# Row maxima, GLA scores and SSD scores and state products as pairs of 64-row products on the two halves of TensorE's contraction rows

## The chip, the core and the metric

One core of one Trainium2 chip runs the whole program in one launch. The metric is the device time of one execution in microseconds (us). The time before is 1848.38 us, the median of 3 runs (1847.5 to 1854.49).

The core has a matrix engine (TensorE: PE for its products, PEld for the loads of its stationary operand), a vector engine (DVE), an activation engine (ACT), GpSimd (POOL), and a queue that issues most of the DMAs (SP). TensorE contracts over up to 128 partitions ("rows") and writes into PSUM, which has eight banks of 512 fp32 columns per partition.

## The reference

Two layers of a hybrid trunk are computed for 128 context tokens and 1024 latent tokens, nine tiles of 128 tokens in all. Each layer makes one wide input projection, feeds four head groups with it, concatenates their outputs and makes one output projection. Three of the groups matter here:

```python
# A: grouped-query attention, 4 query heads on 2 key heads, head dim 64
s = jnp.einsum('bqhgd,bkhd->bhgqk', qblk, k) * scale
p = jax.nn.softmax(s, axis=-1)
# B: gated linear attention (GLA), 4 heads, dk 32, chunked, one scan per direction
att = jnp.where(mask, jnp.einsum('bnihd,bnjhd->bnhij', q_dec, k_in), 0.0)
# D: Mamba-2 SSD, 4 heads in 2 groups, state 64, chunked, one scan per direction
scores = jnp.einsum('bnigs,bnjgs->bnijg', cc, bc)
y_intra = jnp.einsum('bnijg,bnijgr,bnjgrp->bnigrp', scores, decay_ij, xc)
y = jnp.einsum('bigs,bgrps->bigrp', c_n, h) * jnp.exp(cum_n)[..., None]   # state product
```

Group C is a latent attention (MLA) with four heads of width 96. A softmax does not change when the same number is taken from all scores of a row, so the number that stands in for the row's maximum need not be exact.

## The kernel before, in words

Per layer the program projects (the helpers `proj_tok` and `proj_T`, whose products all stand on L245), then runs an attention stage, then the output projection (also L245, tile `op`). In the projections each operand is split into a high and a low part in the type fp32r, three products for one.

The attention stage runs eight heads in turn, four GQA and four MLA. While head n goes through `attend` (score products `st` on L1057, exponentials on ACT, value products `po` on L1067 to L1073), the preparation of head n+1 is advanced in small steps. `STEPS` says how many steps belong to a head, and `paced` hangs each step behind the last instruction issued by `attend`. Part of the preparation is `maxima`. For every query tile of 128 tokens it multiplies the query tile with all 1280 keys in three products (512, 512 and 256 columns, L710, tile `mx`), and DVE reduces each product to a maximum (L711). Nine tiles make 25 products for one head, 200 for the GQA heads of both layers and 200 for the MLA heads. The GQA products contract over 128 rows: the high part of the query on 64 rows and its low part on the other 64, against the high part of the key, which stands twice in `KA`. Head 0 is prepared earlier, between the tiles of the last projection (`cons_qk`, tiles `psP`).

Beside the heads run four more streams, whose instructions are written before the heads: two GLA scans (`gla`), the SSD state scans (`ssd_states`) and the SSD outputs (`ssd_out`). For the four GLA heads of 32 rows each, POOL spreads the query into four masked copies (L853, `g_Qb`), and one 128-row product of 512 columns in plain fp32 makes the scores (L865, `att`); DVE copies them under the causal mask (L867). For the two SSD groups POOL masks `C` in two copies (L962, `d_cb`); one product of 256 columns makes the scores (L987, `dsc`), and two of 256 columns multiply `C` with the carried states of both directions (L996, `dyi`), which DVE scales (L1001) and POOL adds.

The order on each engine comes from a scheduler of the programming layer. It lays the instructions of all streams out before the run, by its own estimate of when each could start; on the chip every engine takes its own in that order. PSUM is given out by tags: `psA`, `psB` two banks each, `psC` one, `psD` three. The maxima of head 0 and all GLA and SSD products use `psD`, the other maxima `psA`.

Of the kernel before, what the change touches and what calls it, by code (L numbers as in the profile page):

```python
# [8 lines left out]
F32 = mybir.dt.float32  # L9
# [15 lines left out]
WO_AT, WO_N = 5, 5  # L25
STEPS = (13, 19, 13, 25, 22, 20, 19, 0)
EPS = 1e-6
# [7 lines left out]
def hybrid_trunk_kernel(ctx: ExitStack, tc: tile.TileContext, a):  # L35
# [53 lines left out]
    bm = const.tile([128, 256], F32, name="bm")  # L89
    hm = const.tile([128, 4], F32, name="hm")  # L90

# [242 lines left out]
    for l in range(L):  # L334
# [83 lines left out]
        with st1:  # L418
# [281 lines left out]
            def maxima(sets, mpass, mr, psX=psA):  # L700

                qb = sets[3]
                mx = mxp.tile([128, T, 3], F32, name="mx", tag="mx", bufs=2)
                lt_m, rh_m = mpass
                for t in range(T):
                    s = slice(t * 128, (t + 1) * 128)
                    cks = ((0, 128),) if t == 0 else ((128, 512), (640, 512), (1152, 256))
                    for i, (o, n) in enumerate(cks):
                        p = psX("mx")
                        pe.matmul(p[:, 0:n], lhsT=lt_m[:, s], rhs=rh_m[:, o:o + n], start=True, stop=True)  # L710
                        dve.tensor_reduce(out=mx[:, t, i:i + 1], in_=p[:, 0:n], axis=AX.X, op=ALU.max)  # L711
                    if t not in (0, 4, 8):
                        yield
                        continue
# [20 lines left out]
            def both(xs, ys):  # L735

                for _ in zip_longest(xs, ys):
                    yield

            def prep_gqa(h):  # L740
# [5 lines left out]
                rq = slice((h % 2) * 64, (h % 2) * 64 + 64)  # L746
                rq2 = slice(64 - (h % 2) * 64, 128 - (h % 2) * 64)
                q = qT[:, h // 2, :]
                eng = pool if h else dve

                def rest():
                    for x in QC:
                        act.copy(qb[0:64, x], q[rq, x])
                        yield
# [46 lines left out]
        with ExitStack() as sta:  # L801
# [25 lines left out]
            def gla(d):  # L827
# [3 lines left out]
                for n, t in enumerate([*(range(T - 1, 0, -1) if d else range(1, T)), 0]):  # L831
                    last = n == T - 2
                    if t == 0:
# [17 lines left out]
                                             op0=ALU.mult, op1=ALU.mult)  # L851
                    qb = W([128, 4, 128], f"g_Qb{d}")
                    pool.tensor_tensor(out=qb, in0=kq[:, 128:256].unsqueeze(1).to_broadcast([128, 4, 128]),  # L853
                                       in1=hm.unsqueeze(2).to_broadcast([128, 4, 128]), op=ALU.mult)
                    if not last:
# [11 lines left out]
                    dve.copy_predicated(A, mask[:, d, :].unsqueeze(1).to_broadcast([128, 4, 128]),  # L867
                                        p.rearrange("p (h i) -> p h i", i=128))
                    o = psD("go")
# [40 lines left out]

            gm = W([128, 2], "gm")
            sp.dma_start(out=gm, in_=a["gm"])

            def h_rows(t, d):
# [3 lines left out]
            def ssd_states(d):  # L918
# [5 lines left out]
                for t in [*(range(T - 1, 1, -1) if d else range(1, T - 1)), 0]:  # L924
# [7 lines left out]
                    if t == 0:  # L932
                        hs = W([128, 128], "d_hs", 1, tag="d_yi")
# [14 lines left out]
            def ssd_out():  # L948

                for t in (0, 4, 5, 3, 6, 2, 7, 1, 8):  # L950
# [5 lines left out]
                    sp.dma_start(out=sz, in_=d_sz[t])  # L956
                    Hs = []
                    for d in range(2 if t else 0):
                        Hs.append(W([128, 256], "d_Hb", 2))
                        sp.dma_start(out=Hs[d], in_=h_rows(t, d))  # L960
                    cb = W([128, 2, 128], "d_cb")
                    pool.tensor_tensor(out=cb, in0=bc[:, 1, :].unsqueeze(1).to_broadcast([128, 2, 128]),  # L962
                                       in1=gm.unsqueeze(2).to_broadcast([128, 2, 128]), op=ALU.mult)
                    for d, tr in enumerate((TRI_F, TRI_B)):
# [12 lines left out]
                    for h in range(4):  # L977
# [11 lines left out]
                    dve.tensor_tensor(out=Dm.rearrange("p (g r) i -> p g r i", r=2),  # L989
                                      in0=scp[:, 0:256].rearrange("p (g i) -> p g i", i=128).unsqueeze(2).to_broadcast([128, 2, 2, 128]),  # L990
                                      in1=Dm.rearrange("p (g r) i -> p g r i", r=2), op=ALU.mult)
                    yield
                    if t:
                        ip = psD("dyi")
                        for d in range(2):
                            pe.matmul(ip[:, d * 256:(d + 1) * 256], lhsT=bc[:, 1, :], rhs=Hs[d], start=(d == 0), stop=(d == 1),  # L996
                                      skip_group_check=True)
                        for d in range(2):
                            yi = W([128, 256], "d_yi")
                            e = d * 36 + t * 4  # L1000
                            dve.tensor_tensor(out=heads(yi), in0=heads(ip[:, d * 256:(d + 1) * 256]),  # L1001
                                              in1=ec[:, e:e + 4].unsqueeze(2).to_broadcast([128, 4, 64]), op=ALU.mult)
                            pool.tensor_tensor(out=y, in0=y, in1=yi, op=ALU.add)
                    yp = psD("dy")
# [108 lines left out]
            def prep_mla(h):  # L1113
# [65 lines left out]

                yield from both(maxima((ka, kb, qa, qb), (qb[0:96], ka[0:96]), 96), rest())  # L1180

# [125 lines left out]
def _constants(np):  # L1307
# [12 lines left out]
    hd = i // 32  # L1320
# [3 lines left out]
    def rope(rot):  # L1324
# [18 lines left out]
        "sel": np.tile(np.eye(2, dtype=np.float32), (2, 1)),  # L1343
        "hm": (hd[:, None] == np.arange(4)[None, :]).astype(np.float32),
        "gm": ((i // 64)[:, None] == np.arange(2)[None, :]).astype(np.float32),
        "rope": np.concatenate([c64, s64, c32, s32], axis=1),
# [89 lines left out]
```

## Time and profile before

| | us |
|---|---|
| median of 3 runs | 1848.38 (1847.5 to 1854.49) |
| profiled execution, its own time | 1848.65 |
| its span, first to last instruction | 1846.8 |
| PE busy | 1720.3 (93%) |
| DVE busy | 1191.8 (65%) |
| ACT busy | 867.2 (47%) |
| POOL busy | 740.6 (40%) |

Matmuls are pipelined: a product's row in the trace lasts from its start to the modelled end of its result, longer than it keeps the engine from the next one. What it costs the engine is the distance from its start to the start of the next. A plain fp32 product shows as two rows, an fp32r product as one.

### The profile page before, as it was taken

What the parts mean: (1) busy time and instruction counts of PE and PEld (TensorE: products, weight loads), DVE (VectorE), ACT (ScalarE), POOL (GpSimd) and SP (SyncE); (2) the same over time, 40 slices, a digit from 0 to 9 for tenths busy, and PEclk for the clock granted to TensorE, in tenths of its full rate; (3) what the DMA queues carried; (4) which work ended last, traced back from release to release, by engine and by line L of the source; (5) the groups of instructions that cost most, each with busy time, mean ns of one, the idle gap of its engine ahead of it and who ended that gap; (6) DMA issues with size and microseconds to landing.
All of it is one profiled execution on the core that took longest, in us unless ns stands there. A gap on an engine that the chain in (4) does not pass through costs nothing.

```text
span 1846.8 us, 25193 instructions
## 1 busy us (share of the span) xinstructions
PE 1720.3 (93%) x8200; PEld 1321.0 (72%) x8200; DVE 1191.8 (65%) x2302; ACT 867.2 (47%) x1914; POOL 740.6 (40%) x911
## 2 busy tenths in 40 slices
PE   6999989999999998999999999999999999999998
PEld 2787977887665666656777999889666666665676
DVE  7627888566877887782455357543686878677233
ACT  5634422433654665583443152232465477557322
POOL 4633238852444444330334323771344454333011
PEclk9999998999999999999999999999998999899999
DMA  8434453333332331142434332131332232114243
GB/s 290 134 97 139 140 158 90 106 111 99 109 99 73 87 97 49 38 149 60 143 118 129 99 101 86 56 101 43 111 117 84 68 98 86 46 38 149 80 143 114
DMA packets 179684, 190.99 MB, mean 103 GB/s; under 512 B 29406, under 2 KB 140720, under 8 KB 179552
## 3 DMA queue, kind: packets, MB, share of 16 engines
q1 hardware_dynamic: 174208, 179.11, 31.9%
q10 hardware_dynamic: 5344, 10.26, 1.8%
q8 instruction: 65, 1.06, 0.2%
q14 instruction: 67, 0.55, 0.1%
HBM read 141.00 MB, written 48.30 MB: 103 GB/s over the span
## 4 chain that ended last, share of the span: by engine, by line
PE 36%; DVE 11%; DMA 7%; POOL 4%; ACT 3%; issue 3%; SPq 0%; POOLq 0%; DVEq 0%; ACTq 0%
PE psP L245 11%; PE op L245 8%; PE st L1057 3%; PE po L1073 3%; DVE mx L711 2%; DMA R<-d_rec 2%; PE mx L710 1%; DVE Pl L1065 1%; DMA d_rec<-rc 1%; PE po L1069 1%; DMA wst<-in_w_in_dram 1%; PE po L1067 1%; PE po L1068 1%; POOL ss L107 1%; POOL sq L577 1%
## 5 line engine op out<-in xcount | busy, mean ns | idle before, releaser
L711 DVE TENSOR_REDUCE mx<-mx 128x1 f32<-128x512 f32 (+2 forms) x400 | 224.5, 582 | 93.6 <-PE mx L710 92.0
L245 PE MATMUL psP<-whi,hh 128*128 128x512 f32 (+2 forms) x576 | 204.9, 366 | 5.6 <-DVE whi L235 4.3
L245 PE MATMUL psP<-wlo,hh 128*128 128x512 f32 (+2 forms) x576 | 204.8, 363 | 3.4 <-POOL wlo L239 2.8
L245 PE MATMUL psP<-whi,hl 128*128 128x512 f32 (+2 forms) x576 | 188.4, 360 | 0.0
L239 POOL TENSOR_TENSOR wlo<-wst,whi 128x512 fp32r<-128x512 f32 (+3 forms) x106 | 128.9, 1224 | 141.5 <-DVE whi L235 82.4
L245 PE MATMUL psP<-hh,whi 128*128 128x384 f32 x480 | 163.0, 339 | 4.7 <-DVE whi L235 3.7
L1057 PE MATMUL st<-QA,KA 128*128 128x512 f32 (+1 forms) x336 | 165.2, 492 | 0.6 <-DVE Pl L1065 0.4
L245 PE MATMUL psP<-hl,whi 128*128 128x384 f32 x480 | 160.2, 335 | 0.0
L245 PE MATMUL psP<-hh,wlo 128*128 128x384 f32 x480 | 155.0, 337 | 0.1
L1065 DVE TENSOR_TENSOR Pl<-st,Ph 128x512 fp32r<-128x512 f32 x160 | 109.7, 686 | 67.2 <-ACT st L1063 66.0
L1062 ACT ACTIVATE Ph<-st 128x512 fp32r<-128x512 f32 x160 | 95.5, 597 | 111.2 <-PE st L1057 104.4
L1072 ACT ACTIVATE P<-st 128x512 f32<-128x512 f32 (+1 forms) x176 | 99.7, 567 | 74.4 <-PE st L1057 65.3
L1057 PE MATMUL st<-QB,KB 66*128 66x512 f32 (+3 forms) x336 | 133.2, 401 | 0.0
L245 PEld LDWEIGHTS psP<-wlo,hh 128*128 128x128 f32 x576 | 111.5, 195 | 21.3 <-POOL wlo L239 6.8
L245 PEld LDWEIGHTS psP<-whi,hh 128*128 128x128 f32 x576 | 111.6, 195 | 20.0 <-DVE whi L235 6.1
L245 PEld LDWEIGHTS psP<-whi,hl 128*128 128x128 f32 x576 | 109.5, 194 | 12.0
L1057 PEld LDWEIGHTS st<-QA,KA 128*128 128x128 f32 x336 | 65.8, 196 | 50.2 <-issue 39.8
L245 PEld LDWEIGHTS psP<-hh,whi 128*128 128x128 f32 x480 | 90.1, 188 | 11.9 <-DVE whi L235 5.6
L1057 PE MATMUL st<-QB,KA 96*128 96x512 f32 (+1 forms) x168 | 93.6, 557 | 2.2 <-ACT P L1072 1.8
L1063 ACT ACTIVATE st<-st 128x512 f32<-128x512 f32 x160 | 94.9, 593 | 0.0
L235 DVE CAST whi<-wst 128x512 fp32r<-128x512 f32 (+3 forms) x114 | 74.0, 662 | 31.8 <-DMA wst<-in_w_in_dram 19.2
L1073 PE MATMUL po<-P,vm 128*65 128x512 f32 (+1 forms) x176 | 88.9, 587 | 4.6 <-ACT P L1072 2.3
(361 smaller groups left out, 4315.6 us busy)
## 6 DMA issues: line engine op xcount, KB each, us to landing
ast<-in_w_ada_dram SPq DMA_DIRECT2D x96, 256.0 KB
wst<-in_w_in_dram SPq DMA_DIRECT2D x64, 256.0 KB
wost<-in_w_out_dram SPq DMA_DIRECT2D x16, 512.0 KB
d_xs<-d_xb SPq DMA_DIRECT2D x32, 192.0 KB
ot<-d_oT SPq DMA_DIRECT2D x18, 320.0 KB
d_tok<-vv SPq DMA_DIRECT2D x18, 256.0 KB
d_gt<-gg SPq DMA_DIRECT2D x24, 192.0 KB
g_qk<-d_qk SPq DMA_DIRECT2D x36, 128.0 KB
```

Of the source, the lines that this page charges most:

```text
L107: pool.tensor_tensor(out=rs, in0=rs, in1=mhalf[:, 0:c], op=ALU.pow)
L235: dve.tensor_copy(hi[:, 0:n], st[:, 0:n])
L239: eng.tensor_tensor(out=lo[:, 0:n], in0=st[:, 0:n], in1=hi[:, 0:n], op=ALU.subtract)
L245: pe.matmul(p, lhsT=lt, rhs=rh, start=(first and i == 0), stop=(last and i == n - 1))
L577: pool.tensor_tensor(out=ws_[:, :, x, :].rearrange("p (h y) f -> p h y f", y=2), in0=zs[:, :, 1 - x, :].rearrange("p (h y) f -> p h y f", ...
L711: dve.tensor_reduce(out=mx[:, t, i:i + 1], in_=p[:, 0:n], axis=AX.X, op=ALU.max)
L1057: anchors["pe"] = pe.matmul(sp_[:, 0:nq], lhsT=kx[:, ks], rhs=qx[:, qs], start=(i == 0), stop=(i == len(spasses) - 1))
L1062: act.activation(out=Ph[:, 0:nq], in_=sp_[:, 0:nq], func=AF.Exp, scale=scale)
L1063: anchors["act"] = act.activation(out=sp_[:, 0:nq], in_=sp_[:, 0:nq], func=AF.Exp, scale=scale)
L1065: anchors["dve"] = dve.tensor_tensor(out=Pl[:, 0:nq], in0=sp_[:, 0:nq], in1=Ph[:, 0:nq], op=ALU.subtract)
L1072: anchors["act"] = act.activation(out=P[:, 0:nq], in_=sp_[:, 0:nq], func=AF.Exp, scale=scale)
L1073: pe.matmul(po[0:65, 0:nq], lhsT=v[:, kt, vi, :], rhs=P[:, 0:nq], start=(j == 0), stop=last, skip_group_check=True)
```

## The change

The GQA maxima no longer use the low part of the query. The query's high part now stands twice, on rows 0 to 63 (in `QB`) and on rows 64 to 127 (in `QA`), and the low part moves to rows 0 to 63 of `QA`. Two query tiles, t and t+1, are multiplied in turn with the same key columns, one on the lower 64 rows of the array, the other on the upper 64, each into a bank of its own. Tile 0 stays alone, on 64 rows. The preparation yields more often, so `STEPS` grows from 13, 19, 13 to 17, 23, 17. The MLA maxima stay as they were.

The GLA scores become two products of 64 rows and 256 columns, one for heads 0 and 1 and one for heads 2 and 3, in two `psD` banks; the masked copies shrink from four to two, and the masked copy on DVE is made in two halves. The SSD scores become two products of 64 rows and 128 columns, one for each group, in two `psD` banks; the state products are 64 rows by 256 columns and go into the same banks. The mask `gm` and the copies `d_cb` go, one DVE multiplication of 512 columns becomes two of 256, and the scalings by `ec` become four of 128 columns instead of two of 256.

```diff
-STEPS = (13, 19, 13, 25, 22, 20, 19, 0)
+STEPS = (17, 23, 17, 25, 22, 20, 19, 0)
...
 def maxima(sets, mpass, mr, psX=psA):
-                        p = psX("mx")
-                        pe.matmul(p[:, 0:n], lhsT=lt_m[:, s], rhs=rh_m[:, o:o + n], start=True, stop=True)
-                        dve.tensor_reduce(out=mx[:, t, i:i + 1], in_=p[:, 0:n], axis=AX.X, op=ALU.max)
...
+                    elif t % 2:
+                        for i, (o, n) in enumerate(cks):
+                            pp = [psX("mx") for _ in mpass]
+                            for j, (lt_m, rh_m) in enumerate(mpass):
+                                pe.matmul(pp[j][:, 0:n], lhsT=lt_m[:, (t + j) * 128:(t + j + 1) * 128], rhs=rh_m[:, o:o + n],
+                                          start=True, stop=True)
+                            for j, p in enumerate(pp):
+                                dve.tensor_reduce(out=mx[:, t + j, i:i + 1], in_=p[:, 0:n], axis=AX.X, op=ALU.max)
+                            if i < 2:
+                                yield
...
 def prep_gqa(h):
                 for x in QC:
-                    act.copy(qa[rq, x], q[rq, x])
-                    eng.tensor_tensor(out=qa[rq2, x], in0=q[rq, x], in1=qa[rq, x], op=ALU.subtract)
+                    act.copy(qb[0:64, x], q[rq, x])
+                    act.copy(qa[64:128, x], q[rq, x])
+                    eng.tensor_tensor(out=qa[0:64, x], in0=q[rq, x], in1=(qa[64:128, x] if h % 2 else qb[0:64, x]), op=ALU.subtract)
                     yield
-                yield from both(maxima(sets, (qa, ka), 64, psA if h else psD), rest())
+                yield from both(maxima(sets, ((qb[0:64], ka[0:64]), (qa[64:128], ka[64:128])), 64, psA if h else psD), rest())
...
 def gla(d):
-                    p = psD("att")
-                    pe.matmul(p, lhsT=kq[:, 0:128], rhs=qb.rearrange("p h i -> p (h i)"), start=True, stop=True)
+                    pp = [psD("att") for _ in range(2)]
+                    for i, p in enumerate(pp):
+                        r = slice(i * 64, i * 64 + 64)
+                        pe.matmul(p[:, 0:256], lhsT=kq[r, 0:128], rhs=qb[r].rearrange("p h i -> p (h i)"), start=True, stop=True)
...
 def ssd_out():
-                    scp = psD("dsc")
-                    pe.matmul(scp[:, 0:256], lhsT=bc[:, 0, :], rhs=cb.rearrange("p g i -> p (g i)"), start=True, stop=True)
+                    gp = [psD("dsc") for _ in range(2)]
+                    for g, p in enumerate(gp):
+                        r = slice(g * 64, g * 64 + 64)
+                        pe.matmul(p[:, 0:128], lhsT=bc[r, 0, :], rhs=bc[r, 1, :], start=True, stop=(t == 0), skip_group_check=True)
+                    if t:
+                        for g, p in enumerate(gp):
+                            r = slice(g * 64, g * 64 + 64)
+                            pe.matmul(p[:, 128:384].rearrange("p (d c) -> p d c", c=128), lhsT=bc[r, 1, :],
+                                      rhs=Hs[r, :, g * 128:(g + 1) * 128], start=False, stop=True, skip_group_check=True)
...
```

Since the order is the scheduler's, the change moves more than it writes. On PE, in the projection in which head 0 is prepared (first layer), this stood before; `mx` is a maximum's product, `psP` a product of the projection:

```order
L245 MATMUL psP<-hh,whi 128x384
L710 MATMUL mx<-KA_3695,QA_3697 128x512
L245 MATMUL psP<-hl,whi 128x384
L245 MATMUL psP<-hh,wlo 128x384
L710 MATMUL mx<-KA_3695,QA_3697 128x512
L245 MATMUL psP<-hh,whi 128x384
```

and this stands there now, where `QB` marks the product on the lower half of the rows and `QA` its partner on the upper half:

```order
L245 MATMUL psP<-hh,whi 128x384
L718 MATMUL mx<-KA_3695,QB_3698 128x512
L245 MATMUL psP<-hl,whi 128x384
L245 MATMUL psP<-hh,wlo 128x384
L245 MATMUL psP<-hh,whi 128x384
L245 MATMUL psP<-hl,whi 128x384
L245 MATMUL psP<-hh,wlo 128x384
L245 MATMUL psP<-hh,whi 128x384
L718 MATMUL mx<-KA_3695,QA_3697 128x512
L245 MATMUL psP<-hl,whi 128x384
L245 MATMUL psP<-hh,wlo 128x384
L718 MATMUL mx<-KA_3695,QB_3698 128x256
```

The two products of a pair stand six 128-row products apart, and the next pair's first follows two products later. On PE in the attention stage of the first layer, where head 1 is prepared under head 0's scores (`st`) and values (`po`), this stood before (`dU` is an SSD state product of 128 rows, `QA_4311` the query of head 1):

```order
L1057 MATMUL st<-QA_3697,KA_3695 128x512
L1057 MATMUL st<-QB_3698,KB_3696 128x512
L710 MATMUL mx<-KA_3695,QA_4311 128x512
L931 MATMUL dU<-d_xw,d_xs_4389 128x256
L710 MATMUL mx<-KA_3695,QA_4311 128x512
L1067 MATMUL po<-Ph,vh 65x512
```

and this stands there now, with `QB_4312` for the lower half and `att` for the two GLA score products:

```order
L718 MATMUL mx<-KA_3695,QB_4312 128x256
L942 MATMUL dU<-d_xw,d_xs_4447 128x256
L1083 MATMUL po<-Pl,vh 65x512
L1087 MATMUL po<-P,vg 65x512
L1071 MATMUL st<-QA_3697,KA_3695 128x512
L1071 MATMUL st<-QB_3698,KB_3696 128x512
L718 MATMUL mx<-KA_3695,QA_4311 128x256
L1081 MATMUL po<-Ph,vh 65x512
L1082 MATMUL po<-Ph,vl 64x512
L878 MATMUL att<-g_Qb_4410,g_kq_4407 128x256 x2
L1083 MATMUL po<-Pl,vh 65x512
```

The `mx` pair is parted by five products of the full array, while this pair of `att` has stayed together. Over the whole program the products that use at most 64 rows stood in 32 unbroken stretches on PE before, and stand in 275 now.

## Rows read from the trace of the kernel before

**Rows 1.** The page: the span, and PE's busy time, share and instructions.

```profile
span 1846.8 us, 25193 instructions
PE 1720.3 (93%) x8200; PEld 1321.0 (72%) x8200; DVE 1191.8 (65%) x2302; ACT 867.2 (47%) x1914; POOL 740.6 (40%) x911
```

**Rows 2.** The chain that ended last, its shares of the span by engine.

```profile
PE 36%; DVE 11%; DMA 7%; POOL 4%; ACT 3%; issue 3%; SPq 0%; POOLq 0%; DVEq 0%; ACTq 0%
```

**Rows 3.** Busy time by stretch: stretch, length, engines, granted clock, DMA share, GB/s.

```profile
396.00:446.00 50.00, 45.51 (x247) 40.64 (x246) 25.78 (x48) 12.04 (x26) 9.22 (x13) 1.00 0.24 76
446.00:720.00 274.00, 256.60 (x1169) 173.53 (x1170) 222.00 (x523) 167.47 (x373) 121.83 (x148) 0.98 0.30 88
720.00:860.00 140.00, 129.62 (x551) 86.28 (x550) 87.49 (x170) 82.16 (x158) 37.44 (x38) 0.98 0.25 79
1318.00:1600.00 282.00, 265.79 (x1193) 179.96 (x1194) 226.82 (x530) 169.06 (x377) 121.79 (x149) 0.96 0.30 86
```

**Rows 4.** PE's waits for other engines, by line: us, times, longest.

```profile
PEld mx L710 <- DVE mx L711: 27.2, 35, 3.4
PEld po L1069 <- DVE Pl L1065: 26.7, 30, 3.4
...
PEld po L1073 <- ACT Ou L1084: 10.6, 12, 1.9
PEld mT L727 <- DVE m L724: 10.5, 8, 3.2
...
PEld kT L857 <- DVE g_kq L849: 7.9, 12, 1.5
```

**Rows 5.** Timeline of PE in the projection with head 0's maxima: start, duration, instruction.

```profile
430.90 0.28 PE L710 MATMUL mx<-KA,QA 128*128 128x256 f32 x1
431.01 0.34 PE L245 MATMUL psP<-hh,wlo 128*128 128x384 f32 x1
...
431.71 0.40 PE L710 MATMUL mx<-KA,QA 128*128 128x512 f32 x1
431.95 0.34 PE L245 MATMUL psP<-hh,whi 128*128 128x384 f32 x1
```

**Rows 6.** Timeline of PE: one GLA score product, two rows merged.

```profile
563.88 1.02 PE L865 MATMUL att<-g_Qb,g_kq 128*128 128x512 f32 x2
```

**Rows 7.** L865: durations min/median/max in ns, first and last start.

```profile
L865 PE MATMUL att<-g_Qb,g_kq x72: 590/592/1061, 471.5 to 1594.6; 128*128 128x512 f32 x72
```

**Rows 8.** Timeline of PE where one 64-row product stands between 128-row products.

```profile
371.03 0.34 PE L245 MATMUL psP<-c1l,whi 128*128 128x384 f32 x1
371.20 0.34 PE L245 MATMUL psP<-c1h,wlo 128*128 128x384 f32 x1
371.38 0.34 PE L245 MATMUL psP<-c2s,whi 128*128 128x384 f32 x1
371.65 0.44 PE L245 MATMUL psP<-c2s,wlo 64*128 64x384 f32 x1
372.02 0.44 PE L245 MATMUL psP<-c1h,whi 128*128 128x384 f32 x1
372.30 0.34 PE L245 MATMUL psP<-c1l,whi 128*128 128x384 f32 x1
```

**Rows 9.** Timeline of PE: three 64-row products in a row.

```profile
366.66 0.79 PE L245 MATMUL psP<-c2s,wlo 64*128 64x384 f32 x3
```

**Rows 10.** Groups by line and shape: count, busy us, mean ns, idle before.

```profile
L711 DVE TENSOR_REDUCE mx<-mx 128x1 f32<-128x512 f32 x256 | 171.4, 684 | 51.7 <-PE mx L710 50.9
L711 DVE TENSOR_REDUCE mx<-mx 128x1 f32<-128x256 f32 x128 | 53.2, 416 | 32.1 <-PE mx L710 31.5
L853 POOL TENSOR_TENSOR g_Qb<-g_kq,hm 128x512 f32<-128x512 f32 x36 | 39.0, 1083 | 33.9 <-DVE g_kq L850 33.3 <-PE st L1057 0.3
L962 POOL TENSOR_TENSOR d_cb<-d_bc,gm 128x256 f32<-128x256 f32 x18 | 11.0, 613 | 19.0 <-DMA d_bc<-d_bc 18.8
L989 DVE TENSOR_TENSOR d_D<-dsc,d_D 128x512 f32<-128x512 f32 x18 | 12.3, 681 | 0.1
```

More of the change, by code (lines that the diff above doesn't have):

```diff
@@ L89, in hybrid_trunk_kernel @@
     bm = const.tile([128, 256], F32, name="bm")
-    hm = const.tile([128, 4], F32, name="hm")
+    hm = const.tile([128, 2], F32, name="hm")
     def load_constants(pl):
@@ L703, in maxima @@
                 mx = mxp.tile([128, T, 3], F32, name="mx", tag="mx", bufs=2)
-                lt_m, rh_m = mpass
                 for t in range(T):
-                    s = slice(t * 128, (t + 1) * 128)
                     cks = ((0, 128),) if t == 0 else ((128, 512), (640, 512), (1152, 256))
-                    for i, (o, n) in enumerate(cks):
-                        p = psX("mx")
-                        pe.matmul(p[:, 0:n], lhsT=lt_m[:, s], rhs=rh_m[:, o:o + n], start=True, stop=True)
-                        dve.tensor_reduce(out=mx[:, t, i:i + 1], in_=p[:, 0:n], axis=AX.X, op=ALU.max)
+                    if len(mpass) == 1 or t == 0:
+                        s = slice(t * 128, (t + 1) * 128)
+                        lt_m, rh_m = mpass[0]
+                        for i, (o, n) in enumerate(cks):
+                            p = psX("mx")
+                            pe.matmul(p[:, 0:n], lhsT=lt_m[:, s], rhs=rh_m[:, o:o + n], start=True, stop=True)
+                            dve.tensor_reduce(out=mx[:, t, i:i + 1], in_=p[:, 0:n], axis=AX.X, op=ALU.max)
+                    elif t % 2:
+                        for i, (o, n) in enumerate(cks):
+                            pp = [psX("mx") for _ in mpass]
[6 more added lines that the diff above has]
+                                yield
                     if t not in (0, 4, 8):
-                        yield
+                        if len(mpass) == 1 or t % 2 == 0:
+                            yield
                         continue
@@ L851, in gla @@
                                              op0=ALU.mult, op1=ALU.mult)
-                    qb = W([128, 4, 128], f"g_Qb{d}")
-                    pool.tensor_tensor(out=qb, in0=kq[:, 128:256].unsqueeze(1).to_broadcast([128, 4, 128]),
-                                       in1=hm.unsqueeze(2).to_broadcast([128, 4, 128]), op=ALU.mult)
+                    qb = W([128, 2, 128], f"g_Qb{d}")
+                    pool.tensor_tensor(out=qb, in0=kq[:, 128:256].unsqueeze(1).to_broadcast([128, 2, 128]),
+                                       in1=hm.unsqueeze(2).to_broadcast([128, 2, 128]), op=ALU.mult)
                     if not last:
@@ L863, in gla @@
                     yield
-                    p = psD("att")
-                    pe.matmul(p, lhsT=kq[:, 0:128], rhs=qb.rearrange("p h i -> p (h i)"), start=True, stop=True)
+                    pp = [psD("att") for _ in range(2)]
+                    for i, p in enumerate(pp):
+                        r = slice(i * 64, i * 64 + 64)
+                        pe.matmul(p[:, 0:256], lhsT=kq[r, 0:128], rhs=qb[r].rearrange("p h i -> p (h i)"), start=True, stop=True)
                     A = Az[d]
-                    dve.copy_predicated(A, mask[:, d, :].unsqueeze(1).to_broadcast([128, 4, 128]),
-                                        p.rearrange("p (h i) -> p h i", i=128))
+                    for i, p in enumerate(pp):
+                        dve.copy_predicated(A[:, 2 * i:2 * i + 2], mask[:, d, :].unsqueeze(1).to_broadcast([128, 2, 128]),
+                                            p[:, 0:256].rearrange("p (h i) -> p h i", i=128))
                     o = psD("go")
@@ L908, in gla @@
                     put_oT(2, t, sq)
-            gm = W([128, 2], "gm")
-            sp.dma_start(out=gm, in_=a["gm"])
             def h_rows(t, d):
@@ L956, in ssd_out @@
                     sp.dma_start(out=sz, in_=d_sz[t])
[L957 to L963, printed above, removed]
+                    if t:
+                        Hs = W([128, 2, 256], "d_Hb")
+                        for d in range(2):
+                            sp.dma_start(out=Hs[:, d, :], in_=h_rows(t, d))
                     for d, tr in enumerate((TRI_F, TRI_B)):
@@ L992, in ssd_out @@
-                    yield
[L993 to L1003, printed above, removed]
+                    gp = [psD("dsc") for _ in range(2)]
@@ new lines, in ssd_out @@
+                    dve.tensor_tensor(out=Dm, in0=Dm, in1=DT, op=ALU.mult)
+                    for g, p in enumerate(gp):
+                        x = Dm[:, 2 * g:2 * g + 2, :]
+                        dve.tensor_tensor(out=x, in0=p[:, 0:128].unsqueeze(1).to_broadcast([128, 2, 128]), in1=x, op=ALU.mult)
+                    if t:
+                        yi = W([128, 2, 4, 64], "d_yi")
+                        for g, p in enumerate(gp):
+                            for d in range(2):
+                                e = d * 36 + t * 4 + 2 * g
+                                dve.tensor_tensor(out=yi[:, d, 2 * g:2 * g + 2, :], in0=heads(p[:, 128 + d * 128:256 + d * 128]),
+                                                  in1=ec[:, e:e + 2].unsqueeze(2).to_broadcast([128, 2, 64]), op=ALU.mult)
+                        for d in range(2):
+                            pool.tensor_tensor(out=heads(y), in0=heads(y), in1=yi[:, d], op=ALU.add)
@@ L1178, in rest @@
                         yield
-                yield from both(maxima((ka, kb, qa, qb), (qb[0:96], ka[0:96]), 96), rest())
+                yield from both(maxima((ka, kb, qa, qb), ((qb[0:96], ka[0:96]),), 96), rest())
             def run_mla(h):
```

13 lines of the change are left out of this document (3 added, 10 removed).

## The prediction, made before the changed kernel ran

> **What bounds the kernel now.** I read the page first. PE is busy for 93% of the span and DVE for 65% [rows 1], and of the chain that ended last 36% is PE's against 11% for DVE and 4% for POOL [rows 2]. PE sets the time, but not everywhere alike, so the table by stretches comes next [rows 3]. In the projection with head 0's maxima (396 to 446 us) PE is nearly full and DVE half idle. In the attention stage, 446 to 720 us and again from 1318 us in the second layer, DVE is busy for 222 of 274 us, 81%, while PE's rows cover 257 of 274. PE's share there is flattered by modelled ends, so I took its waits by line [rows 4]. The five largest that belong to the attention stage sum to 27.2 + 26.7 + 10.6 + 10.5 + 7.9 = 82.9 us over both layers, four of them on DVE. So in the projection a delay of PE is a delay of the end, and in the attention stage PE and DVE take turns: a delay of PE there may shorten a wait of PE further on, by at most 82.9 us in all.
>
> **What a product costs.** The reader should look at starts, not durations. A maximum's product of 512 columns starts at 431.71 and the next product at 431.95, so it costs 0.24 us; one of 256 columns costs 0.11 us [rows 5]. Neither disturbs the 128-row products beside it. A GLA score shows as two rows that together last 1.02 us, the second with its 0.59 us [rows 6, 7], so one row costs 1.02 - 0.59 = 0.43 us and the product 0.86 us. By columns, the new pieces cost as much in sum as the old whole if each runs alone: two GLA products of 256 columns again 0.86, and the same for the SSD products and for the maxima, which keep their columns. If the two halves of a pair run at once, the shorter one is free.
>
> **What a change between 128 and 64 rows costs.** The kernel before already has such places. One 64-row product stands between 128-row products of equal columns [rows 8]: 371.20 to 371.38 is an ordinary distance (0.17 to 0.18), then come 0.27 before the 64-row product, 0.37 after it, and 0.28 until the array is back in step. From 371.38 to 372.30 that is 0.92 us for three distances which ordinarily take 3 x 0.175 = 0.525, so one lone 64-row stretch costs 0.395 us extra. It is the change that costs, not the 64 rows: three such products in a row take 0.79 us with the last one's tail [rows 9], 0.79 - 0.33 = 0.46 from the first start to the third, so all but the first of them run at the ordinary distance.
>
> **The sum, part by part.**
>
> Stretches. The new order has 275 stretches of at most 64 rows, 32 were there before, so 243 are new; 172 of them hold a single product. 35 stand directly behind a product of the projection in which head 0 is prepared, where PE waits for nothing: 35 x 0.395 = 13.8 us, all of it on the path. The other 208 stand in the attention stage: 208 x 0.395 = 82.2 us of PE time.
>
> Overlap. Only where products on opposite halves are neighbours can they run at once. The order has 50 such neighbours: 25 of two maxima (0.11 to 0.24 us to gain), 11 of two GLA scores (0.43), 14 of others (0.11 to 0.43). That is 9 to 17 us, about 12. No row of before shows a product on the upper half, so the ends are nothing and -17; I take -8, near the middle. What a step from one half to the other costs is not shown either: between nothing, as for equal products in rows 9, and half a stretch, 0.2 us, or 10 us in all. I take nothing, since rows 9 are nearest to it.
>
> The Trainium skill speaks on both points, and against each other. "TensorE: Matmul & The Clock Gate", in Part 3 (packing small matmuls), has products on different row groups start about 4 ns apart; by it the overlap would be the whole 12 us and the sum below 4 us less. "TensorEngine Tiling (Array Packing)", under Key Properties, has the engine drained whenever the tiling mode changes but not when only the tile does; rows 8 show a stall at each change of mode, 0.395 us for two, and no run here shows a change of tile.
>
> What the waits take up. The 82.2 - 8 = 74.2 us of PE time in the attention stage are laid against waits of 82.9 us. The ends are all taken up (0) and nothing (74). A late PE also makes DVE late, since DVE stood idle 50.9 and 31.5 us for the maxima's products [rows 10], and then PE's own waits for DVE do not shrink. I take half, 37 us.
>
> DVE. It gets 36 + 18 + 32 = 86 instructions more from the splits in two. A reduction of 512 columns takes 684 ns and one of 256 takes 416 [rows 10], so 268 ns are for 256 columns and 148 ns for the instruction: 86 x 0.148 = 12.7 us. DVE is free for a fifth of that stage and will wait more for PE, so I take a quarter, 3 us; the ends are 0 and 12.7.
>
> POOL. Half of the 39.0 us of `g_Qb` and the 11.0 us of `d_cb` go [rows 10], 30.5 us. POOL waits in both for its input and has 4% of the chain: I take -3, with ends 0 and -30. The SP queue loses two DMAs of `gm`; it issues them once per layer, worth nothing. The six casts on ACT for a query stand in another order with the same count: nothing.
>
> PSUM banks. The GLA pair and the SSD pair each hold two of the three `psD` banks where one was held, and the SSD pair keeps them until DVE has scaled the states (one of its products before took 681 ns, rows 10). Behind a PE product that waits for a bank stand the scores of the running head, and ACT waits for those. Bounds: nothing, up to 54 pairs x 0.68 = 37 us. I take nothing, because the order was laid out with these banks, and leave it in the range.
>
> The sum is 13.8 + 37 + 3 - 3 = 51 us. The profiled execution took 1848.65 us (span 1846.8 and 1.85 around it), within 0.3 us of the median, so the forecast is 1848.65 + 51, about 1900 us.
>
> **Rivals.**
>
> The waits swallow it. If each delay of PE in the attention stage only shortens a later wait for DVE, 13.8 - 3 = 11 us remain: 1860 us. For it speaks that 74 is less than 82.9; against it, that DVE waits for PE as often as PE for DVE.
>
> The full bill. Nothing is taken up, nothing overlaps, and DVE's share shows: 13.8 + 82.2 + 12.7 = 109, 1957 us. The wait for banks would lead the same way: 51 + 37, 1937 us.
>
> Faster. The stall of rows 8 is an exposed operand load behind a drained array. If a half's load could go in beside the work of the other rows, no stretch would cost anything, the 12 us of overlap and POOL's 3 would be gained, and the time would be 1834 us. This decides as soon as the price of a stretch is under 15 / 243 = 0.06 us. Against it stand all lone stretches before: their price is far above. Only their upper-half kin are unseen.
>
> The pairs do not do what they say because they are parted, and yet the order is better for other reasons (fewer POOL steps in the GLA chain); the stalls and those gains cancel: no change, 1848 us. This needs 30 us from POOL, all of it on the path, and most of the stalls taken up.
>
> **How the numbers follow.** Forecast, between 1875 and 1925: 0.66. Swallowed, about 1860: 0.12. Full bill or banks, 1925 to 1957: 0.10. Faster, about 1834: 0.07. No change: 0.05. What a measurement of this kernel can tell from no change is about 0.5%, 9 us, so 1839 to 1858 counts as the same. Of the swallowed case a tenth falls there: slower 0.66 + 0.10 + 0.11 = 0.87, same 0.06, faster 0.07. The range goes from 1860 to 1940 and leaves out the faster cases and the top of the full bill. The likeliest case's own range is 1875 to 1925.
>
> **What would show it.** Timelines of PE should show 0.27 and 0.37 us around each lone `mx`, `att` or `dsc` product, and two neighbours on opposite halves starting a few hundredths apart (overlap) or 0.24 and 0.43 apart (none). The stretch from 396 to 446 should grow by about 7 us in each layer, the attention stage by about 18, the other projections and the output projection by nothing. DVE's wait for `mx` should grow. The forecast is wrong if lone half products follow each other at ordinary distances, if PE's waits for DVE fall by as much as the stalls rise, or if the granted clock, 0.96 to 1.00 now [rows 3], drops in the stage with more stalls.

## The result: 1913.5 us, 3.6% slower

The changed kernel takes 1913.47 us (median of 4 runs, 1903.98 to 1921.69), the kernel before, run beside it, 1847.94 us (4 runs, 1844.18 to 1854.49). The ratio is 1.0362, 95% interval 1.033 to 1.0394. The forecast was 1900 us, within 1860 to 1940. So sign and cause have to be tested, and 13 us are missing.

### The profile page after: what moved, and what is told of

The parts are those of the page before. It is cut to its first block, busy times and chain, and to the rows that moved or that the text cites. A ratio compares the mean times of both kernels' runs of the same rounds, so it can differ in the third digit from the quotient of the medians.

```text
span 1908.6 us, 25451 instructions
## 1 busy us (share of the span) xinstructions
PE 1789.4 (94%) x8308; PEld 1316.8 (69%) x8308; DVE 1199.8 (63%) x2388; ACT 872.2 (46%) x1914; POOL 712.9 (37%) x893
## 4 chain that ended last, share of the span: by engine, by line
PE 38%; DVE 6%; DMA 4%; POOL 3%; ACT 2%; issue 2%; SPq 0%; POOLq 0%; ACTq 0%; DVEq 0%
PE psP L245 12%; PE op L245 8%; PE st L1071 4%; PE po L1087 3%; PE mx L718 1%; PE po L1083 1%; PE att L878 1%; PE po L1081 1%; PE po L1082 1%; DVE mx L712 1%; POOL ss L107 1%; PE go L900 1%; PE mx L711 1%; DMA wst<-in_w_in_dram 1%; DMA R<-d_rec 1%
## 5 line engine op out<-in xcount | busy, mean ns | idle before, releaser
L721 DVE TENSOR_REDUCE mx<-mx 128x1 f32<-128x512 f32 (+1 forms) x192 | 112.6, 598 | 76.2 <-PE mx L718 75.2
L712 DVE TENSOR_REDUCE mx<-mx 128x1 f32<-128x512 f32 (+2 forms) x208 | 113.7, 570 | 35.5 <-PE mx L711 34.7
L1087 PE MATMUL po<-P,vg 128*65 128x512 f32 (+1 forms) x176 | 91.7, 604 | 4.2 <-ACT Ou L1098 3.5
```

Source lines behind the costliest of these rows:

```text
L721: dve.tensor_reduce(out=mx[:, t + j, i:i + 1], in_=p[:, 0:n], axis=AX.X, op=ALU.max)
L1087: pe.matmul(po[0:65, 0:nq], lhsT=v[:, kt, vi, :], rhs=P[:, 0:nq], start=(j == 0), stop=last, skip_group_check=True)
```

## The profile after

Span, busy times and the chain's shares, against [rows 1, 2]:

```profile
span 1908.6 us, 25451 instructions
...
PE 1789.4 (94%) x8308; PEld 1316.8 (69%) x8308; DVE 1199.8 (63%) x2388; ACT 872.2 (46%) x1914; POOL 712.9 (37%) x893
...
PE 38%; DVE 6%; DMA 4%; POOL 3%; ACT 2%; issue 2%; SPq 0%; POOLq 0%; ACTq 0%; DVEq 0%
```

The span grew by 61.8 us and PE's busy time by 69.1; DVE has 8.0 us more work, POOL 27.7 less. The chain moved from DVE (11% to 6%) to PE. PE in the projection with head 0's maxima, changed kernel, to be read by its starts:

```profile
397.55 0.34 PE L245 MATMUL psP<-hh,wlo 128*128 128x384 f32 x1
397.81 0.49 PE L718 MATMUL mx<-KA,QB 64*128 64x512 f32 x1
397.82 0.49 PE L718 MATMUL mx<-KA,QA 64*128 64x512 f32 x1
398.24 0.45 PE L245 MATMUL psP<-hh,whi 128*128 128x384 f32 x1
398.52 0.34 PE L245 MATMUL psP<-hl,whi 128*128 128x384 f32 x1
...
400.98 0.34 PE L245 MATMUL psP<-hh,whi 128*128 128x384 f32 x1
401.24 0.50 PE L718 MATMUL mx<-KA,QB 64*128 64x512 f32 x1
401.67 0.44 PE L245 MATMUL psP<-hl,whi 128*128 128x384 f32 x1
401.95 0.33 PE L245 MATMUL psP<-hh,wlo 128*128 128x384 f32 x1
...
402.93 0.50 PE L718 MATMUL mx<-KA,QA 64*128 64x512 f32 x1
403.35 0.44 PE L245 MATMUL psP<-hl,whi 128*128 128x384 f32 x1
```

The first pair stayed together. Its two products start 3 ns apart in the trace (printed as 0.01) and the next product comes 0.42 us later, as behind a lone one: the second product is free. The next pair was parted, and each half pays by itself: 0.26 us ahead, 0.43 behind, then 0.28, instead of 0.17, 0.24 and 0.17. That is the stall of [rows 8], 0.39 us, and QA's, on the upper rows, is the same as QB's on the lower. The weight loads show it too:

```profile
397.37 0.19 PEld L245 LDWEIGHTS psP<-hh,wlo 128*128 128x128 f32 x1
397.81 0.18 PEld L718 LDWEIGHTS mx<-KA,QB 64*128 64x128 f32 x1 [0.25 <-issue]
```

The load for the 128-row product at 397.55 started 0.18 us ahead of it, beside the product before. The load for the 64-row product starts only with its product, at 397.81.

The layers, from the first maximum of one to that of the next, and to the end; before, then after (stretch, length, engines, granted clock, DMA share, GB/s):

```profile
396.35:435.25 38.90, 38.90 (x222) 37.11 (x221) 15.50 (x32) 4.91 (x11) 0.84 (x1) 1.00 0.13 47
1269.26:1306.96 37.70, 37.70 (x218) 36.90 (x218) 15.51 (x32) 4.72 (x10) 0.00 (x0) 1.00 0.12 43
396.35:1269.26 872.91, 828.96 (x4018) 644.10 (x4017) 545.45 (x1083) 410.03 (x919) 342.07 (x435) 0.98 0.30 92
1269.26:1846.83 577.57, 535.77 (x2367) 380.28 (x2366) 371.08 (x786) 288.48 (x619) 183.41 (x228) 0.96 0.30 92
```

```profile
392.12:437.72 45.60, 45.60 (x220) 36.50 (x220) 16.08 (x32) 4.98 (x11) 0.99 (x1) 1.00 0.11 40
1311.93:1356.43 44.50, 44.50 (x218) 36.39 (x218) 16.08 (x32) 4.72 (x10) 0.00 (x0) 1.00 0.10 36
392.12:1311.93 919.81, 873.27 (x4072) 648.21 (x4071) 545.12 (x1126) 412.29 (x919) 329.13 (x426) 0.97 0.29 87
1311.93:1908.63 596.70, 561.54 (x2421) 372.70 (x2420) 379.86 (x829) 290.38 (x619) 169.32 (x219) 0.97 0.30 89
```

The first two rows of each are the projections with head 0, one a layer: 38.9 to 45.6 and 37.7 to 44.5 us, PE full in all. The first layer grew by 46.9 us, the second by 19.1. They differ mostly by the clock: summed over its records, the lower level (1.2 GHz) was granted in the first layer for 27.3 us before and 61.4 now, in the second for 44.5 and 35.3. The largest piece lies in this stretch of 25 us, at a mean clock of 0.59 and with 9.0 us of work for DVE:

```profile
515.00:540.00 25.00, 21.90 (x49) 10.92 (x49) 9.00 (x20) 6.02 (x12) 1.64 (x3) 0.59 0.27 73
```

In it the lower level was granted for 20.5 us without a break, from 518.3. This is what PE and then POOL did ahead of that:

```profile
513.88 0.80 PE L1071 MATMUL st<-QA,KA 128*128 128x512 f32 x1
518.10 1.09 PE L942 MATMUL dU<-d_xw,d_xs 128*128 128x256 f32 x2 [3.42 <-POOL d_xw L939]
519.12 1.22 PE L878 MATMUL att<-g_Qb,g_kq 64*128 64x256 f32 x2
```

```profile
517.02 0.45 POOL L1113 TENSOR_TENSOR gt<-gt,R 128x128 f32<-128x128 f32 x1 [5.98 <-DMA R<-d_rec]
517.43 0.61 POOL L939 TENSOR_TENSOR d_xw<-d_xs,wdt 128x256 f32<-128x256 f32 x1
```

PE stood idle for 3.42 us, waiting for the scaled inputs `d_xw` of an SSD state product. POOL's `d_xw` was queued behind `gt`, which had waited 5.98 us for the reciprocals `R` from a DMA.

PE's waits in the weight-load queue, against [rows 4]:

```profile
PEld mx L718 <- issue: 20.3, 64, 0.9
PEld mx L711 <- DVE mx L712: 19.1, 22, 2.6
...
PEld po L1083 <- DVE Pl L1079: 17.7, 21, 3.6
...
PEld att L878 <- issue: 11.8, 30, 1.4
PEld mx L718 <- DVE mx L721: 10.2, 22, 3.2
```

The maxima's wait for DVE (27.2) is now 19.1 + 10.2 = 29.3, that for `Pl` fell from 26.7 to 17.7. The stall at a change of row count has no releaser; in the load queue it appears as "issue" on L718 and L878. DVE's side, against [rows 10]:

```profile
L721 DVE TENSOR_REDUCE mx<-mx 128x1 f32<-128x512 f32 x128 | 86.9, 687 | 58.9 <-PE mx L718 58.1
L712 DVE TENSOR_REDUCE mx<-mx 128x1 f32<-128x512 f32 x128 | 85.5, 683 | 21.1 <-PE mx L711 20.6
...
L881 DVE COPY_PREDICATED g_A<-tri,att 128x256 f32<-128x256 int32 x72 | 30.5, 439 | 14.4 <-PE att L878 14.0
```

For the same 256 reductions of 512 columns DVE now waits 58.1 + 20.6 = 78.7 us for PE, where it was 50.9.

## The experiments

To take the clock apart from the work, the table also multiplies each execution's time by its own mean granted clock: the time if all ran at the upper level (2.4 GHz). This takes out slightly too much, since a wait is no longer at a low clock: over the changed kernel's 16 runs 0.001 of clock went with 1.7 us, not 1.9. The last column and the text compare means. Intervals are 95% by the normal law, so somewhat too narrow for the kernels with four runs. "Before" pools its 35 runs beside the experiments (three chips, means 1843.4 to 1845.0), "changed" its 4 + 6 + 6 runs; each ratio is to the runs of before beside it.

| kernel | us, median | ratio to before | clock | us x clock | against before |
|---|---|---|---|---|---|
| before | 1844.3 | 1 | 0.969 | 1787.4 | 0 |
| changed | 1914.9 | 1.0362 [1.033, 1.0394] | 0.963 | 1842.2 | +54.7 ± 1.8 |
| e1, single 64-row maxima | 1890.2 | 1.0244 [1.0202, 1.0285] | 0.970 | 1832.4 | +45.0 ± 1.3 |
| e2, all on 128 rows | 1848.2 | 1.001 [0.9986, 1.0034] | 0.971 | 1793.0 | +5.6 ± 2.3 |
| e3, pairs bound | 2368.9 | 1.2846 [1.2797, 1.2895] | 0.838 | 1985.9 | +198 |
| e4, scan pairs bound | 1960.8 | 1.0634 [1.059, 1.0678] | 0.943 | 1848.5 | +61 |
| e5, maxima part alone | 1898.2 | 1.0287 [1.0259, 1.0315] | 0.965 | 1831.4 | +44.0 ± 2.1 |
| e6, scan part alone | 1856.5 | 1.0066 [1.0043, 1.0088] | 0.970 | 1800.7 | +13.3 ± 4.1 |
| e7, lower half only | 1920.8 | 1.042 [1.0395, 1.0444] | 0.963 | 1850.7 | +63.3 ± 3.5 |
| e9, one scaling on DVE | 1908.9 | 1.035 [1.0315, 1.0384] | 0.964 | 1839.5 | +52.1 ± 1.9 |

**e1: the switches without the pairs.** Kernel before, one line, with `rq` the half of the rows that the head's query is in. The order on PE stays word for word; 163 new stretches, no pairs, no other banks.

```diff
-                yield from both(maxima(sets, (qa, ka), 64, psA if h else psD), rest())
+                yield from both(maxima(sets, (qa[rq], ka[rq]), 64, psA if h else psD), rest())
```

> The kernel before, with one edit: each GQA maximum contracts over 64 rows only (the query's high part), one product at a time as before, same banks, and the instructions stand in the same order on PE. It has 163 new 64-row stretches, 36 of them directly behind a product of the projection. Theory (each change of the row mode stalls PE, 0.395 us for a lone stretch): 36 x 0.395 = 14 us in full and half of 127 x 0.395 = 50, so 1848 + 39 = about 1887 us (1870 to 1913), with 0.27 us before a lone product and 0.43 us from its start to the next. Rival (the loss of the change comes from its banks, its order or its parted pairs, not from the 64 rows): 1848 us, within 5.

Measured: 1890.22 us, 44 more. The projection with head 0 took 46.3 and 44.9 us where it was 38.9 and 37.7, 14.6 in sum against 36 x 0.395 = 14.2. The clock is that of before (0.970), so this is the switches' price alone. Since the order is the same, each distance between two starts on PE can be set against its own before. From the first maximum on, the profiled execution is 42.8 us longer: the distances at the new stretches (into, inside and the two behind) grew by 52.2 us, those in which PE waited 0.06 us or more in either execution shrank by 10.5, those at the lower clock grew by 1.1, and the rest did not change.

**e2: the pairs without the switches.** Changed kernel with its banks, steps and splits, and every new product on 128 rows (the GLA and SSD products then mix heads and groups).

```diff
-                        pe.matmul(p[:, 0:256], lhsT=kq[r, 0:128], rhs=qb[r].rearrange("p h i -> p (h i)"), start=True, stop=True)
+                        pe.matmul(p[:, 0:256], lhsT=kq[:, 0:128], rhs=qb.rearrange("p h i -> p (h i)"), start=True, stop=True)
...
```

> The changed kernel, with all its new products over the 128 rows: pairs, banks, yields and steps stay as changed, no product changes the row mode. The GLA scores then mix two heads and the SSD products two groups, which leaves the separation of heads out of the output. Theory (stalls): the loss goes, 1848 us (1838 to 1862), PE waits for nothing new. Rival (banks, order, steps): it stays, 1890 us or more, with waits of PE for DVE at att, dsc and mx.

Measured: 1848.16 us, no difference. Banks, DVE's 86 instructions, POOL's relief and the new order come to nothing in sum; at full clock to +5.6. The clock (0.971) is not lower than before.

**e3 and e4: pairs bound.** The products of a pair were put into a section that the scheduler doesn't part, in the whole changed kernel (e3) or in its GLA and SSD part on the kernel before (e4).

```diff
-                    for i, p in enumerate(pp):
+                    with tc.tile_critical():
+                      for i, p in enumerate(pp):
```

> The changed kernel, with the two products of each pair (four of an SSD tile) bound together so that nothing stands between them on PE. 136 new stretches instead of 243, 14 of them behind a product of the projection, and 166 neighbours on opposite halves, worth 44.6 us if they overlap fully. Theory (stalls and overlap): 136 x 0.395 = 53.7 - 44.6 = 9 us of PE time, less than that on the path: 1855 us (1845 to 1868). Rival (a pair that must wait for two free banks at once holds up PE): 1885 us or more, with long waits of PE for DVE in front of mx.

> The kernel before with only the GLA and SSD part of the change, its products bound together as in the run with pairs together; the maxima are those of before. 54 new stretches, 70 neighbours on opposite halves: 54 x 0.395 = 21.3 - 26.3 = -5 us of PE time, 3 us less for POOL and 3 more for DVE: 1844 us (1835 to 1855). Rival (two of three psD banks held by a pair make the scans and then PE wait): 1860 us or more.

Measured: 2368.85 and 1960.82 us, both expectations missed. The loss is far above that of the changed kernel, whose pairs are not bound. PE in e4:

```profile
462.96 0.40 PE L710 MATMUL mx<-KA,QA 128*128 128x512 f32 x1
464.09 0.70 PE L869 MATMUL att<-g_Qb,g_kq 64*128 64x256 f32 x4 [0.73 <-DMA d_hs<-d_H]
464.88 0.44 PE L1075 MATMUL po<-Pl,vh 128*65 128x512 f32 x1
```

```profile
PEld att L869 <- issue: 66.4, 36, 6.2
PEld dsc L990 <- issue: 30.7, 18, 4.3
```

Ahead of each section PE goes through semaphore instructions and a branch, and behind it a drain (54 branches and 57 drains on PE in e4, none and 3 in the changed kernel). The loss is 115 us in 54 sections, 2.1 us each, and 3.5 us each in the 150 sections of e3; about half of it in e4 and more in e3 goes with the lower clock. The times are those of the rivals, and how much is the section itself and how much a wait for two free banks, these runs don't separate: the waits ahead of the pairs show as "issue", up to 6.2 us long in e4, which names no releaser. So neither run tells what a pair costs that is bound for nothing.

**e5 and e6: the two parts apart.** e5 is the changed kernel with the GLA and SSD products as before, e6 with the maxima as before; of each, the line that stays undone:

```diff
# e5
-                    pp = [psD("att") for _ in range(2)]
+                    p = psD("att")
...
# e6
-                yield from both(maxima(sets, ((qb[0:64], ka[0:64]), (qa[64:128], ka[64:128])), 64, psA if h else psD), rest())
+                yield from both(maxima(sets, (qa, ka), 64, psA if h else psD), rest())
...
```

> The kernel before with the row maxima of the GQA heads alone made into pairs of 64-row products; the GLA scores and the SSD products stay as they were. The order holds 166 new 64-row stretches, 36 of them beside the projection, and 33 neighbours on opposite halves. Theory (each stretch costs its two changes of row count, at full price beside the projection and about half elsewhere): 36 x 0.395 = 14.2, and (130 x 0.395 - 5.8 for the overlaps) / 2 = 23, so about 37: 1885 us, between 1875 and 1897; the stretch of layer 0 with the projection grows by about 7 us, as it does with the whole change, and the granted clock stays near 0.97. Rival 1 (the scores and scans carry most of the loss, because they stand on the chain of layer results): 1860 us or less. Rival 2 (the clock falls with the maxima's stalls too): over 1897, at a granted clock under 0.965.

> The kernel before with the GLA scores and the SSD score and state products alone made into pairs of 64-row products; the maxima stay as they were. The order holds 91 new stretches, none beside the projection, and 19 neighbours on opposite halves. Theory (half the price of 91 stretches less the overlaps): (91 x 0.395 - 7.1) / 2 = 14, so 1861 us, between 1853 and 1870; the projection with head 0 is as long as before, and the granted clock is near 0.97. Rival 1 (the parts add up to the whole change only together with the fall of the clock, which the scans cause): 1875 us or more, at a clock under 0.965. Rival 2 (overlap pays for the stalls here, since these products are the long ones): 1848 us or less.

Measured: e5 1898.15 us, 13 above the expectation and 1 above its range, at a clock of 0.965: just where its second rival begins; e6 1856.50, inside its own. At full clock they add up, 44.0 + 13.3 = 57.3 against 54.7 ± 1.8 for the whole, with 37 and 14 expected. The projection is as in the theory: in e5 45.5 and 44.5 us, in e6 as before. This is e6:

```profile
389.03:427.92 38.89, 38.89 (x221) 37.10 (x221) 15.51 (x32) 4.95 (x11) 0.64 (x1) 1.00 0.13 47
1282.93:1320.63 37.70, 37.70 (x218) 36.90 (x218) 15.50 (x32) 4.73 (x10) 0.00 (x0) 1.00 0.12 42
```

So the maxima bring three quarters of the loss. Of e5's 53 us, 9 ± 7 go with a lower clock, which neither e1, with nearly as many stretches, nor e2, with the pairs on full rows, has; why paired 64-row maxima should lower it and single ones not was not tried.

**e7: no overlap.** Changed kernel, all new products on the lower 64 rows, PE's order the same.

```diff
-                        r = slice(i * 64, i * 64 + 64)
+                        r = slice(0, 64)
...
```

> The changed kernel with every new product on the lower 64 rows instead of one on each half, so that nothing can overlap; the order of the instructions on TensorE is word for word the same, and so is the count of changes of row count. Heads and groups are mixed in the GLA and SSD products, so these outputs leave the separation of heads out. Theory (neighbours on opposite halves run at once, 12 us in all, of which the waits take up about half): 1919 us, 6 above the changed kernel run beside it, between 3 and 12 above; neighbours that started a few ns apart now start 0.24 us (256 columns at 128-byte rows of maxima) to 0.43 us (GLA scores) apart. Rival 1 (the overlap is worth nothing to the end): within 2 us of the changed kernel. Rival 2 (a step from one half to the other costs like a change of row count): 5 us or more under the changed kernel.

Measured: 1920.83 us; against the changed kernel 8 us more by the means (at full clock 8.5 ± 3.6), 4 by the medians of the runs beside each other (e8: 1916.47). The pair from above, in e7, and the GLA pair in the changed kernel and in e7:

```profile
396.88 0.34 PE L245 MATMUL psP<-hh,wlo 128*128 128x384 f32 x1
397.14 0.73 PE L718 MATMUL mx<-KA,QB 64*128 64x512 f32 x2
397.80 0.44 PE L245 MATMUL psP<-hh,whi 128*128 128x384 f32 x1
```

```profile
477.25 0.70 PE L878 MATMUL att<-g_Qb,g_kq 64*128 64x256 f32 x4
477.88 0.44 PE L1083 MATMUL po<-Pl,vh 128*65 128x512 f32 x1
```

```profile
477.23 1.13 PE L878 MATMUL att<-g_Qb,g_kq 64*128 64x256 f32 x4
478.29 0.45 PE L1083 MATMUL po<-Pl,vh 128*65 128x512 f32 x1
```

Two maxima hold PE for 0.66 us instead of 0.43, two GLA scores for 1.06 instead of 0.63. The overlap is real: between PE's starts, waits and lower clock aside, it is worth 13 us, and to the end 4 to 8. A step from one half to the other costs nothing that shows.

**e8: the changed kernel again.** No edit.

> The changed kernel once more, unaltered, for a second profile of it and more of its times beside its clock. Theory 1 (the clock's fall belongs to the kernel: TensorE's work is cut into more pieces): the new profile's granted clock is again 0.965 or less against 0.970 of the kernel before, and the longer runs are those with the lower clock, about 2 us for 0.001. Theory 2 (the one long stretch at half clock behind the wait for d_xw was an accident of one execution): the new profile lacks it, its clock is near 0.970 and its time near 1900 us. Either way the time should be 1904 to 1922 us.

Measured: 1916.47 us (6 runs), clock 0.959 to 0.970. The profile has 17.1 us at half clock from 516.9, again around a wait for `d_xw` (3.54 us); a third one, taken beside e9, has 20.5 us from 514.0. Three profiles of three agree, and so does that of e7 (17.1 us from 518.1), so the stretch belongs to the kernel (theory 1).

**e9: take that wait away.** The one `d_xw` behind `gt` is done by DVE.

```diff
-                    pool.tensor_tensor(out=heads(xw), in0=heads(xb[:, 0:256]),
+                    (dve if (l, d, t) == (0, 0, 7) else pool).tensor_tensor(out=heads(xw), in0=heads(xb[:, 0:256]),
```

> The changed kernel with one instruction moved: the d_xw of layer 0 that stands on POOL behind gt (which waits 6 us for R) is done by DVE, so that the product dU behind it need not wait 3.4 us for it. The order on TensorE is the same but for 2 products that go ahead of two others. In both profiles of the changed kernel, half the clock was granted for 20.5 and 17.1 us right behind that wait, and for 3.4 us at this place before the change. Theory 1 (that wait brings the long stretch at half clock, some 15 us more of it, so 7 to 8 us): the wait and the stretch go (7 us or less at half clock between 505 and 545 us), the granted clock is about 0.004 higher, and the time is 7 to 11 us under the changed kernel beside it: about 1905 us. Theory 2 (the clock follows the mean activity, and a stretch not taken here is taken elsewhere): the stretch goes or shrinks, but the granted clock of the whole run stays at 0.960 to 0.963 and the time within 4 us. Theory 3 (another wait, for R or for dU's neighbours, takes the place of this one): the stretch of 17 us or more is still there.

> The changed kernel, unaltered, on the same chip as the run with one scaling on DVE, to compare with it and for a third profile: 1916 us between 1902 and 1925, clock 0.958 to 0.967, and again a stretch of 14 us or more at half clock behind the wait of dU near 518 us.

Measured: 1908.89 us, the changed kernel beside it (e10) 1913.07. First 40 us of e9 around the place, then 25 of e10, and e9's product `dU`:

```profile
505.00:545.00 40.00, 37.33 (x153) 21.12 (x152) 26.62 (x72) 21.77 (x49) 11.20 (x14) 1.00 0.31 85
```

```profile
512.00:537.00 25.00, 23.10 (x53) 11.60 (x54) 9.53 (x21) 6.01 (x12) 2.06 (x4) 0.59 0.24 69
```

```profile
513.76 0.67 PE L942 MATMUL dU<-d_xw,d_xs 128*128 128x256 f32 x2 [0.78 <-DVE d_xw L939]
```

The wait fell to 0.78 us and the half clock is gone from there, while e10 has it. What it brought to the end is not settled: 5.5 ± 6.7 us by the means, on a clock 0.0015 higher where 0.004 was expected. So without the wait that stretch doesn't come (theory 3 falls), and between theories 1 and 2 the runs don't decide. In the whole profiled execution the lower level was granted for 133 us in e9, for 143, 159 and 153 in the three profiles of the changed kernel, and for 115 before.

The wait alone isn't enough either. e2, with no new change of row count, has the same wait, here with the 25 us behind it:

```profile
505.77 0.70 PE L942 MATMUL dU<-d_xw,d_xs 128*128 128x256 f32 x2 [3.37 <-POOL d_xw L939]
505.77:530.77 25.00, 25.00 (x108) 17.83 (x108) 17.73 (x36) 13.62 (x29) 8.02 (x9) 0.93 0.31 93
```

Behind it the lower level was granted for 3.4 us, not for 17 to 20; in e6, which waits there for 3.36 us, for 3.4 us as well; and e5, which waits for 2.79 us, has none there. So the long stretch came only where the wait and both parts of the change came together; why, no run shows.

## Why the prediction was right, and what it missed

**Stalls.** The step that decided was right: it is the change of row count that costs, 0.395 us a lone stretch. e2 removes the changes and the loss goes; e1 makes only the changes and 44 of the 66 us by which the changed kernel stood over the one beside it are there. In e1 a lone stretch away from waits and the lower clock costs 0.37 us in the mean (114 of them).

**Projection.** Forecast about 7 us a layer, measured 6.7 and 6.8: price and path are right where PE waits for nothing.

**What the waits take up.** Taken as half, with ends at nothing and all. At full clock 54.7 - 13.5 = 41 us came in the rest, against 37 + 3 - 3. The size is right by luck, as two errors cancel. The order of the changed kernel is nearly that of e2, so their starts can be compared as in e1: in three profiles of the changed kernel the distances at the new stretches grew by 61 to 63 us, 13.5 of them in the projections, and those with waits shrank by 10 to 15. So outside the projections some 49 us of PE time came where 74 were forecast, and 10 to 15 of them were taken up where it was 37. (A stall that falls into a wait is counted with the wait.) Nor was 82.9 us the most that could be taken up: it sums the five largest waits alone. The parts show, too, that the share isn't one number: e6 paid 13.3 of 91 x 0.395 - 7.1 = 28.8 us, 46%, e5 outside the projection 44.0 - 14.2 = 30 of 130 x 0.395 - 5.8 = 45.6, 65%.

**Overlap.** Taken at -8 of 12 us of PE time; measured 13 in PE's starts, and 8.5 ± 3.6 to the end (e7). The Trainium skill's "TensorE: Matmul & The Clock Gate", Part 3, has such neighbours start about 4 ns apart; in the trace the two maxima start 3 ns apart, at 397.815 and 397.818, and the rule holds. What decided here was the way into a pair and out of it.

**DVE, POOL, banks.** DVE's busy time grew by 8.0 us, under the 12.7 of the forecast, and POOL's fell by 27.7 where 30.5 was worked out. To the end, all of it came to between nothing and +5.6 (e2). The wait for banks did not show: e2 has the same banks and no loss.

**Attention stage.** Forecast about 18 us a layer. By the windows above, the layers grew by 46.9 - 6.7 = 40 and 19.1 - 6.8 = 12 us outside the projection, so the forecast is wrong for each. By an estimate that takes half of the time at the lower level as lost, the clock explains most of it: (61.4 - 27.3) / 2 = 17 us more in the first layer and (44.5 - 35.3) / 2 = 5 less in the second. Without this the layers grew by 23 and 17 us.

**The term that was mis-sized** is the granted clock. The sum had it at nothing and named it only as a way to be wrong ("drops in the stage with more stalls"). It fell from 0.969 to 0.963, and this is 0.0065 x 1.7 us per 0.001 = 11 us by the slope of the runs, or 14.6 ± 3.8 by time lost at the lower level; set against e2 as above, the distances at the lower clock grew by 15 to 26 us in the three profiles. Added to 51 it is 1848.65 + 51 + 11 to 15, 1911 to 1915 us. The rival of an even exchange of waits (1860 us) fell with e1, which lost 30 us outside the projections; the faster one with the timeline, since the upper half's stall is the lower's and the load of a half starts only with its product; the one of no change with e2, where the new order, banks and POOL's relief gain nothing; the full bill (1957) lies 44 us off.

## What to carry to other kernels

A 64-row product pays for entering and leaving the half array, so pairs are worth their overlap only while it exceeds the change: here 0.23 us gained for a pair of 512-column maxima, 0.43 for GLA scores, against 0.395 paid, and twice that when the scheduler parts the pair. Count the unbroken stretches in the scheduled order on PE, not the pairs in the source; a long run of half products would pay once. When PE loses time in a stage that alternates with other engines, price the clock too: in the changed kernel a wait of 3 us was followed by up to 20 us at half speed, where without the new changes of row count the same wait was followed by 3.4.

## What the runs showed of the hardware that was not expected

- Keeping instructions together in a section was dear: 2.1 us for each section in e4 and 3.5 in e3, lower clock and any wait for banks included.
- The stall of a change shows as no wait of PE: the modelled ends cover it, and PE reads as busy for all 45.60 us of the projection. It is seen as "issue" on the weight load (20.3 us on L718) and as distance between starts; durations alone (0.49 for 0.40 us) hide most of it.
- One POOL instruction, 0.61 us long and queued behind a wait for a DMA, stood ahead of 17 to 20 us at the lower clock in three profiles of one program, and moving it to DVE took all of that stretch away (e9). With the same wait and no new change of row count, 3.4 us were all (e2).
